# Three more q/k pairs by seven products, weights loaded by diagonals, head copies on ScalarE

## The chip, the cores and the metric

The kernel runs on one core of one Trainium2 chip. The metric is the device time of one execution in microseconds; lower is better. Three runs of the kernel before took 2038.73, 2040.16 and 2040.10 us, median 2040.1. One further execution was recorded by the hardware profiler.

Engines are called as in the profile: PE is TensorE's matrix multiplication and PEld its loading of the stationary operand, DVE is VectorE, ACT is ScalarE, POOL is GpSimd, SP is SyncE, which issues nearly all DMAs here.

## The reference

One layer of a hybrid block on x of 256 tokens by 4096 channels, everything in float32:

```
proj = rms_norm(x, norm_in_g) @ w_in                 # 4096 -> 14336
q, k, v, z_a, a_c, g_c, z_c = split(proj)            # each 2048 wide
y_a = rms_norm(chunked_attention(q, k, v, rel_table)) * silu(z_a)
u   = causal_depthwise_conv(a_c * sigmoid(g_c), w_dw) + b_dw      # 31 taps
y_c = rms_norm(silu(layer_norm(u)) @ w_pw + b_pw) * silu(z_c)
h   = x + concat(y_a, y_c) @ w_out                   # 4096 -> 4096
gate = sigmoid(rms_norm(h) @ w_ple_gate + b_ple_gate)  # 4096 -> 4096
out = rms_norm(h + gate * (p @ w_ple), final_g)
```

Attention has 16 heads of 128 channels; with 256 tokens every query's band of nine chunks of 64 reaches all earlier chunks. Almost all of the arithmetic is in the products with `w_in`, `w_out` and `w_ple_gate`.

## The kernel before

**Float32 by three products.** Each operand of a matmul is split into a high part, which the matmul's type holds exactly, and the rest. For weights `parts_of` (L198) does it: ACT copies the tile into `wh` (L203), DVE subtracts (L204) into `wl`. One product is then three matmuls: high by high, low by high, high by low. The stationary operand is a 128 x 128 block of the activations, the moving one 128 x 512 of the weights.

**Two columns at a time.** `mixed_product` (L326) computes, for both halves of the tokens (128 rows each) and for two weight columns of 512, the sum over 32 blocks of 128 channels, taken as 16 pairs. A list such as `early` (L319) gives the order of the pairs and says which are starred. A plain pair takes four products for each of its two blocks: 8 products, 24 matmuls. A starred pair is computed by a scheme of the Strassen and Winograd kind with seven products (P1 to P7), 21 matmuls. It takes sums of the weights, made on DVE for each pair (`ua`, L425 and L426; `ub`, L429 and L430) and split by `pair_parts` (L307) into `uh` and `ul`, and sums of the activations, made once and kept ("combined pairs", `xS` for x). Four helper sums P1, P5, P6, P7 stand in the temporary PSUM banks (`ps_tmp`, four in all) until the last starred pair of the product; `on_helpers` then adds them up on DVE and ACT (L466 to L470) and frees the banks. The other four sums are in `ps_acc`.

**Stages of the first half.** For g = 0 to 3: `glu_conv(g + 1)` (a and gate columns, then the convolution's taps as small DVE instructions put into a list `later`), `heads(g)` (q and k by one `mixed_product`, transposed by heads; v by `product`, L223; attention). `glu_conv(0)` goes ahead of all this and reads x. In the last group `layer_norm_swish` takes the place of the next `glu_conv`: it puts the layer norm over the convolution's output into `later`, with a mean (L742), a variance (L769) and a spread of the factor (L782) as small matmuls in temporary PSUM banks; the pointwise product then reads its result (`uS`, L798 and L799).

`fill` takes the given number of entries from `later` after each pair (`early_fills`, L322) or each two blocks of a `product` (`fills`). They are DVE's work between the weights' parts.

**Which pairs of x are combined.** Pairs 0, 2, 4 and 6 are combined early and kept in tiles of `upool`. In the last `glu_conv` two more, pairs 8 and 10, are made by `more_combinations` (L678) into tiles of the pool `act`; that product has the order `early_six` (L320). `act` has eight slots, which in the end hold four tiles of convolution output and four `y_a`. The q/k products of all four groups use `early`. With the end of the last group's q/k product the pools of the first half's sums are closed and the room goes to other tiles.

**Buffers.** Weight tiles `wt` have five slots, `wh` and `wl` three each, `uh` and `ul` two each. A load is issued by SP when the slot it takes has been read for the last time. For a starred pair the two loads are the two blocks, each with both columns (`two_columns`, L98): `w0` holds w00 and w01, `w1` holds w10 and w11. Outside the first half's glu and q/k products the two columns lie side by side in memory.

**Order.** Each engine runs its instructions in the order that a planner writes at compile time, by dependencies, program order and its own estimates of durations; where the program pins instructions they stay in program order. Nothing is reordered at run time, but for weight loads of PE.

**The q/k end of a group.** The four results of a q/k product are scaled on DVE (L491), transposed by heads on PE into temporary banks (`to_heads`, L822, L830) and copied out by DVE (L835) into `qT` and `kT`. The scores (L844, L845) read them after that, in the stream of the v product or behind it.

Of the kernel before, what the change touches and what calls it, by code (L numbers as in the profile page):

```python
# [16 lines left out]
P = 128  # L17
# [8 lines left out]
def hybrid_block(  # L26
# [71 lines left out]
    def two_columns(w, kb, col, apart):  # L98
# [4 lines left out]
            ap=[list(rows.ap[0]), [apart, 2], [1, NB]],  # L103
        )

    w_first = [wpool.tile([P, 2, NB], F32, tag="w", name="wt") for _ in range(2)]
    for j, col in enumerate((o_a, o_g)):
        nc.scalar.dma_start(w_first[0][:, j], w_in0[:P, col : col + NB])
# [86 lines left out]
    def part_tiles():  # L195
        return [wpool.tile([P, KC, NB], F32R, tag=tag, name=tag, bufs=3) for tag in ("wh", "wl")]

    def parts_of(wt, kc, tiles=None):  # L198
        if tiles is None:
            tiles = part_tiles()  # L200
        wh, wl = tiles
        made = (
            nc.scalar.copy(wh[:, :kc, :], wt[:, :kc, :]),  # L203
            nc.vector.tensor_tensor(  # L204
                wl[:, :kc, :], wt[:, :kc, :], wh[:, :kc, :].bitcast(F32), ALU.subtract
            ),
        )
        return (wh, wl), made
# [103 lines left out]
    def units(text):  # L312

        return [(int(u.rstrip("*")), u.endswith("*")) for u in text.split()]
# [3 lines left out]
    first = units("0 1 3 5 7 9 11 13 15 2* 8 4* 10 6* 12 14")  # L318
    early = units("1 3 5 7 0* 9 2* 11 4* 13 6* 15 8 10 12 14")  # L319
    early_six = units("1 3 5 7 0* 9 2* 11 4* 13 6* 15 8* 10* 12 14")  # L320

    early_fills = (4, 6, 7, 1, 5, 1, 5, 1, 5, 1, 2, 4, 6, 6, 6, 4)  # L322
    final = units("1 0* 3 2* 5 4* 6* 7 8* 9 10* 12* 11 13 14 15")
    late = units("1 3 5 7 9 11 13 15 0* 2 4* 6 8* 10* 12 14")

    def mixed_product(  # L326
# [67 lines left out]
        for n, (pair, seven) in enumerate(order):  # L394
            if n < done:
                continue
            if ahead:
                ahead(pair)
            wts = []
            for k in range(2):  # L400
                wt = wpool.tile([P, 2, NB], F32, tag="w", name="wt")
                nc.sync.dma_start(wt, two_columns(w, 2 * pair + k, col, apart))
                wts.append(wt)
            if n >= len(order) - n_left:
                for k in range(2):
                    tiles = left[2 * (n - len(order) + n_left) + k]
                    held.append((2 * pair + k, parts_of(wts[k], 2, tiles and tiles())[0]))
                fill(fills[n % len(fills)])
                continue
            if not seven:  # L410
                for k in range(2):
                    add_plain(n, k, *parts_of(wts[k], 2)[0])
                fill(fills[n % len(fills)])
                continue
            begins = not helper
            if begins:
                for name in ("P1", "P5", "P7", "P6"):
                    helper[name] = ps_tmp.tile([P, NB], F32, tag="tmp", name=f"acc_{name}")
                banks.update(helper)
            w0, w1 = wts  # L420
            ua = upool.tile([P, 2, NB], F32, tag="u", name="ua")
            ub = upool.tile([P, 2, NB], F32, tag="u", name="ub")
            plus = partial(nc.vector.tensor_tensor, op=ALU.add)
            w0h, w0l = parts_of(w0, 1)[0]
            plus(ua[:, 0], w0[:, 0], w0[:, 1])  # L425
            plus(ua[:, 1], w0[:, 1], w1[:, 1])  # L426
            uah, ual = pair_parts(ua)
            w1h, w1l = parts_of(w1, 2)[0]
            plus(ub[:, 0], ua[:, 0], w1[:, 1])  # L429
            plus(ub[:, 1], ub[:, 0], w1[:, 0])  # L430
            ubh, ubl = pair_parts(ub)
            first = len(made)

            def s_of(i):
                t, at = comb[pair] if isinstance(comb, dict) else (comb[pair // 4], pair % 4)
                return [t[:, at + i // 2, q, (i % 2) * P : (i % 2 + 1) * P] for q in range(2)]

            k0, k1 = 2 * pair, 2 * pair + 1
            add("P1", block(k0, 0), (w0h[:, 0], w0l[:, 0]), n, True)
            add("P5", s_of(1), (uah[:, 0], ual[:, 0]), n, True)  # L440
            add("P7", s_of(0), (uah[:, 1], ual[:, 1]), n, True)
            add("P2", block(k1, 0), (w1h[:, 0], w1l[:, 0]), n, True)
            add("P3", s_of(3), (w1h[:, 1], w1l[:, 1]), n, True)
            add("P6", s_of(2), (ubh[:, 0], ubl[:, 0]), n, True)
            add("P4", block(k1, 1), (ubh[:, 1], ubl[:, 1]), n, True)
            if begins and on_begin:
                on_begin()
            if begins:
                tc.add_manual_dep(
                    made[first].ins, last_transpose[0].ins.name,  # L450
                    mybir.DependencyInfo(mybir.DependencyClass.NoSync, mybir.DependencyReason.DATA),
                    reason="transposes before the helpers take their banks",
                )
            if n == last_seven:
                on_helpers(helper)
            fill(fills[n % len(fills)])
# [365 lines left out]
    def to_heads(st, name):  # L822

        t = spool.tile([P, GH, T], F32, tag="hd", name=name, bufs=5)
        for pair in range(GH // 2):
            pt = tmp_psum()
            for i in range(2):
                for h in range(NH):
                    b = 2 * pair + i
                    nc.tensor.transpose(  # L830
                        pt[:, i * T + h * P : i * T + (h + 1) * P],
                        st[:, h, b * P : (b + 1) * P],
                        ident,
                    )
            nc.vector.tensor_copy(  # L835
                t[:, 2 * pair : 2 * pair + 2, :], pt.rearrange("q (i t) -> q i t", t=T)
            )
        return t
# [40 lines left out]
    def heads(g):  # L879
        nonlocal more  # L880
        bias = spool.tile([P, GH, T], F32, tag="hd", name="bias", bufs=5)
        span = 2 * MAXR + 1
        nc.sync.dma_start(
            bias,
            bass.AP(
                tensor=rel_table.tensor,
                offset=rel_table.offset + g * GH * span + MAXR + P - (T - 1),
                ap=[[1, P], [span, GH], [1, T]],
            ),
        )  # L890
        nc.gpsimd.memset(bias[: P // 2, :, : P // 2], NEG)
        q, k = scaled_pair(w_in0, o_q + g * NB, o_k - o_q, early, r_x, (4,) if g == n_g - 1 else early_fills)
        qT, kT = to_heads(q, "qT"), to_heads(k, "kT")
        if g == n_g - 1:
            first_sums.close()
            more = pool("more", 4)
        accv = product(w_in0, o_v + g * NB, xT, KD)
        v = spool.tile([P, NH, NB], F32, tag="hd", name="v", bufs=5)
        for h in range(NH):
            nc.scalar.activation(v[:, h, :], accv[h], AF.Identity, scale=r_x[:, h : h + 1])  # L900
        attention(g, qT, kT, v, bias)
# [340 lines left out]
```

## Time and profile before

| | |
|---|---|
| median of three runs | 2040.1 us (2038.73 to 2040.16) |
| the profiled execution | 2040.09 us |
| its span, first to last instruction | 2038.1 us |
| mean granted clock of TensorE | 0.998 |
| ACT busy | 1180.8 us (58%) |
| HBM read | 406.39 MB |

The later stages by their start in the profiled execution: q/k of group 2 at 638 us, its v at 718, q/k of group 3 at 766, its v at 858, the pointwise product at 902, the gated products at 985, `w_out` at 1314, `w_ple_gate` at 1652.

In the profile's rows "out<-in" names the tile written and the tiles read; "x" and a number is a count; then come the busy time, the mean time of one in ns, the idle time of the engine ahead of them and what ended it. In a wait's row stand the waiting instruction, what ended the wait, the sum in us, how often, and the longest. In a timeline or a chain the first number is the start in us and the second the length in us; a row with "x3" joins three instructions. In a row of windows the columns are the stretch, its length, the busy time (and count) of PE, PEld, DVE, ACT and POOL, the granted clock, the DMA queues' mean share and GB/s. The chain follows the work that ended last.

### The profile page before, as it was taken

What the parts mean: (1) busy time and instruction counts of PE and PEld (TensorE: products, weight loads), DVE (VectorE), ACT (ScalarE), POOL (GpSimd) and SP (SyncE); (2) the same over time, 40 slices, a digit from 0 to 9 for tenths busy, and PEclk for the clock granted to TensorE, in tenths of its full rate; (3) what the DMA queues carried; (4) which work ended last, traced back from release to release, by engine and by line L of the source; (5) the groups of instructions that cost most, each with busy time, mean ns of one, the idle gap of its engine ahead of it and who ended that gap; (6) DMA issues with size and microseconds to landing.
All of it is one profiled execution on the core that took longest, in us unless ns stands there. A gap on an engine that the chain in (4) does not pass through costs nothing.

```text
span 2038.1 us, 26014 instructions
## 1 busy us (share of the span) xinstructions
PE 2020.2 (99%) x9112; PEld 1661.5 (82%) x9112; DVE 1892.9 (93%) x2700; ACT 1180.8 (58%) x1522; POOL 15.7 (1%) x19
## 2 busy tenths in 40 slices
PE   9999999999999999999999999999999999999997
PEld 7888888887888888888888887888888888888876
DVE  7999999899989998866999999999999999999998
ACT  7655535554555545565566566676565666655555
POOL 0000000000000000000100000000000000000000
PEclk9999999999999999999999999999999999999999
DMA  8666665666566665656666666676666656666765
GB/s 290 192 196 206 199 191 170 200 195 194 176 195 203 201 185 177 187 187 199 201 207 201 197 211 197 220 237 205 216 200 204 215 185 208 198 220 205 235 206 180
DMA packets 161852, 412.28 MB, mean 202 GB/s; under 512 B 12974, under 2 KB 16190, under 8 KB 161722
## 3 DMA queue, kind: packets, MB, share of 16 engines
q1 hardware_dynamic: 161072, 409.80, 63.6%
q8 instruction: 71, 1.16, 0.2%
q10 hardware_dynamic: 650, 0.84, 0.1%
q14 instruction: 59, 0.48, 0.1%
HBM read 406.39 MB, written 4.19 MB: 201 GB/s over the span
## 4 chain that ended last, share of the span: by engine, by line
PE 87%; DVE 9%; issue 2%; DMA 1%; ACT 1%; POOLq 0%; POOL 0%; ACTq 0%; DVEq 0%
PE acc L369 62%; PE acc_P L369 15%; PE acc L217 7%; DVE wl L204 3%; DVE cv L673 3%; PE tmp_ps L169 1%; DVE ul L204 1%; DMA wt<-in_w_in_dram 1%; PE tmp_ps L845 0%; PE tmp_ps L830 0%; PE tmp_ps L863 0%; DMA wt<-in_w_ple_dram 0%; PE tmp_ps L124 0%; PE tmp_ps L868 0%; DVE z L491 0%
## 5 line engine op out<-in xcount | busy, mean ns | idle before, releaser
L369 PE MATMUL acc<-wh,big_t 128*128 128x512 f32 x3846 | 1192.0, 392 | 1.5 <-DVE z L959 1.5
L203 ACT CAST wh<-wt 128x1024 fp32r<-128x1024 f32 (+1 forms) x737 | 715.7, 981 | 570.3 <-PE acc L369 348.9
L204 DVE TENSOR_TENSOR wl<-wt,wh 128x1024 fp32r<-128x1024 f32 (+1 forms) x737 | 824.7, 1130 | 61.1 <-ACT wh L203 57.2
L369 PEld LDWEIGHTS acc<-wh,big_t 128*128 128x128 f32 x3846 | 719.6, 188 | 150.2 <-ACT wh L203 1.9
L369 PE MATMUL acc<-wl,big_t 128*128 128x512 f32 x1923 | 741.9, 391 | 0.0
L369 PEld LDWEIGHTS acc<-wl,big_t 128*128 128x128 f32 x1923 | 360.6, 188 | 76.1 <-DVE wl L204 1.2
L673 DVE SCALAR_TENSOR_TENSOR cv<-uT,dw,cv 128x255 f32<-128x255 f32 (+20 forms) x480 | 204.6, 460 | 1.3
L203 ACT CAST uh<-ub 128x1024 fp32r<-128x1024 f32 x120 | 126.3, 1052 | 115.7 <-DVE ub L430 104.6
L369 PE MATMUL acc_P<-uh,big_t 128*128 128x512 f32 x594 | 182.2, 392 | 0.1
L217 PE MATMUL acc<-wh,big_t 128*128 128x512 f32 x560 | 173.1, 390 | 0.0
L203 ACT CAST uh<-ua 128x1024 fp32r<-128x1024 f32 x120 | 126.4, 1054 | 72.8 <-DVE ua L426 64.9
L204 DVE TENSOR_TENSOR ul<-ub,uh 128x1024 fp32r<-128x1024 f32 x120 | 146.3, 1219 | 7.0 <-ACT uh L203 5.7
L204 DVE TENSOR_TENSOR ul<-ua,uh 128x1024 fp32r<-128x1024 f32 x120 | 146.1, 1218 | 0.6 <-ACT uh L203 0.2
L369 PEld LDWEIGHTS acc_P<-uh,big_t 128*128 128x128 f32 x594 | 110.1, 188 | 26.2 <-ACT uh L203 4.1
L217 PEld LDWEIGHTS acc<-wh,big_t 128*128 128x128 f32 x560 | 104.8, 188 | 21.5
L369 PE MATMUL acc_P<-ul,big_t 128*128 128x512 f32 x297 | 114.5, 393 | 0.3 <-DVE ul L204 0.2
L217 PE MATMUL acc<-wl,big_t 128*128 128x512 f32 x280 | 109.2, 391 | 0.0
L425 DVE TENSOR_TENSOR ua<-wt 128x512 f32<-128x512 f32 x120 | 82.2, 685 | 22.1 <-DMA wt<-in_w_in_dram 17.3
L426 DVE TENSOR_TENSOR ua<-wt 128x512 f32<-128x512 f32 x120 | 82.0, 684 | 5.9 <-DMA wt<-in_w_in_dram 4.3
L430 DVE TENSOR_TENSOR ub<-ub,wt 128x512 f32<-128x512 f32 x120 | 82.2, 685 | 1.2
L429 DVE TENSOR_TENSOR ub<-ua,wt 128x512 f32<-128x512 f32 x120 | 82.0, 683 | 0.2
L369 PE MATMUL acc<-uh,big_t 128*128 128x512 f32 x240 | 74.4, 390 | 0.0
(223 smaller groups left out, 1423.0 us busy)
## 6 DMA issues: line engine op xcount, KB each, us to landing
wt<-in_w_in_dram SPq DMA_DIRECT2D x447, 512.0 KB, 4.1
wt<-in_w_out_dram SPq DMA_DIRECT2D x128, 512.0 KB, 4.3
wt<-in_w_ple_gate_dram SPq DMA_DIRECT2D x128, 512.0 KB, 4.2
wt<-in_w_pw_dram SPq DMA_DIRECT2D x32, 512.0 KB, 4.5
hc<-in_x_dram SPq DMA_DIRECT2D x8, 512.0 KB, 5.9
wt<-in_w_ple_dram SPq DMA_DIRECT2D x8, 512.0 KB, 4.7
xin<-in_x_dram SPq DMA_DIRECT2D x7, 512.0 KB, 8.2
out_dram<-hc SPq DMA_DIRECT2D x12, 256.0 KB, 2.5
```

What stands on the lines that cost most here:

```text
L169: nc.tensor.transpose(pt[:, i * T + h * P : i * T + (h + 1) * P], src[:, h, b * P : (b + 1) * P], ident,)
L203: nc.scalar.copy(wh[:, :kc, :], wt[:, :kc, :]),
L204: nc.vector.tensor_tensor(wl[:, :kc, :], wt[:, :kc, :], wh[:, :kc, :].bitcast(F32), ALU.subtract),
L217: nc.tensor.matmul(acc, a, b[:, k, :], start=kb == 0 and kind == 0, stop=kb == kblocks - 1 and kind == 2,)
L369: nc.tensor.matmul(banks[name], a, b, start=name not in begun, stop=final and ends[name] == n and kind == 2 and not (left and name in "P2 ...
L425: plus(ua[:, 0], w0[:, 0], w0[:, 1])
L426: plus(ua[:, 1], w0[:, 1], w1[:, 1])
L429: plus(ub[:, 0], ua[:, 0], w1[:, 1])
L430: plus(ub[:, 1], ub[:, 0], w1[:, 0])
L673: nc.vector.scalar_tensor_tensor(cv[:, i, PAD - k :], uT[:, i, : T + k - PAD], dw[:, b, k : k + 1], cv[:, i, PAD - k :], ALU.mult, ALU.add,)
```

## The change

1. The q/k product of group 2 takes the order `early_six` (six starred pairs in place of four), that of group 3 a new order `early_five` (five). They read the combined pairs 8 and 10 that the last `glu_conv` made; group 3 reads only pair 10, so that the tile of pair 8 becomes free for `y_a` of group 2.
2. Group 2's fills are 48 in the q/k product and 48 in the v product, in place of 64 and 32.
3. For starred pairs, in all products, the two loads are diagonals: `wd` holds w00 and w11, `wa` holds w01 and w10. `wd` is split whole (1024 columns), of `wa` only w10 (512). `ua` is made by one addition of 1024 columns, `wd` plus w01 repeated, in place of two of 512. The products come in the order P1, P3, P5, P7, P2, P6, P4 in place of P1, P5, P7, P2, P3, P6, P4. This part is computed with the same values as before.
4. The copies of `qT` and `kT` out of PSUM are made by ACT in place of DVE.

```diff
+    def diagonal(w, pair, col, apart, anti):
+
+        rows = w[2 * pair * P : (2 * pair + 1) * P, :]
+        n = rows.ap[0][0]
+        offset, step = (apart, P * n - apart) if anti else (0, P * n + apart)
+        return bass.AP(
+            tensor=rows.tensor, offset=rows.offset + col + offset,
+            ap=[list(rows.ap[0]), [step, 2], [1, NB]],
+        )
...
-    def parts_of(wt, kc, tiles=None):
+    def parts_of(wt, kc, tiles=None, k0=0):
...
+        ks = slice(k0, kc)
         made = (
-            nc.scalar.copy(wh[:, :kc, :], wt[:, :kc, :]),
+            nc.scalar.copy(wh[:, ks, :], wt[:, ks, :]),
             nc.vector.tensor_tensor(
-                wl[:, :kc, :], wt[:, :kc, :], wh[:, :kc, :].bitcast(F32), ALU.subtract
+                wl[:, ks, :], wt[:, ks, :], wh[:, ks, :].bitcast(F32), ALU.subtract
             ),
         )
...
+    early_five = units("1 3 5 7 0* 9 2* 11 4* 13 6* 15 10* 8 12 14")
...
+    third_fills = (4, 5, 6, 1, 4, 1, 4, 1, 4, 1, 2, 1, 1, 5, 4, 4)
...
-                nc.sync.dma_start(wt, two_columns(w, 2 * pair + k, col, apart))
+                nc.sync.dma_start(
+                    wt,
+                    diagonal(w, pair, col, apart, k) if seven
+                    else two_columns(w, 2 * pair + k, col, apart),
+                )
...
-            w0, w1 = wts
+            wd, wa = wts
...
-            w0h, w0l = parts_of(w0, 1)[0]
-            plus(ua[:, 0], w0[:, 0], w0[:, 1])
-            plus(ua[:, 1], w0[:, 1], w1[:, 1])
+            wdh, wdl = parts_of(wd, 2)[0]
+            plus(ua, wd, wa[:, :1].broadcast_to([P, 2, NB]))
             uah, ual = pair_parts(ua)
-            w1h, w1l = parts_of(w1, 2)[0]
-            plus(ub[:, 0], ua[:, 0], w1[:, 1])
-            plus(ub[:, 1], ub[:, 0], w1[:, 0])
+            wah, wal = parts_of(wa, 2, k0=1)[0]
+            plus(ub[:, 0], ua[:, 0], wd[:, 1])
+            plus(ub[:, 1], ub[:, 0], wa[:, 1])
             ubh, ubl = pair_parts(ub)
...
-            add("P1", block(k0, 0), (w0h[:, 0], w0l[:, 0]), n, True)
+            add("P1", block(k0, 0), (wdh[:, 0], wdl[:, 0]), n, True)
+            add("P3", s_of(3), (wdh[:, 1], wdl[:, 1]), n, True)
             add("P5", s_of(1), (uah[:, 0], ual[:, 0]), n, True)
             add("P7", s_of(0), (uah[:, 1], ual[:, 1]), n, True)
-            add("P2", block(k1, 0), (w1h[:, 0], w1l[:, 0]), n, True)
-            add("P3", s_of(3), (w1h[:, 1], w1l[:, 1]), n, True)
+            add("P2", block(k1, 0), (wah[:, 1], wal[:, 1]), n, True)
...
-            nc.vector.tensor_copy(
+            nc.scalar.copy(
                 t[:, 2 * pair : 2 * pair + 2, :], pt.rearrange("q (i t) -> q i t", t=T)
             )
...
-        q, k = scaled_pair(w_in0, o_q + g * NB, o_k - o_q, early, r_x, (4,) if g == n_g - 1 else early_fills)
+        order, fills = {
+            n_g - 2: (early_six, third_fills), n_g - 1: (early_five, (4,))
+        }.get(g, (early, early_fills))
+        q, k = scaled_pair(w_in0, o_q + g * NB, o_k - o_q, order, r_x, fills)
...
-        accv = product(w_in0, o_v + g * NB, xT, KD)
+        accv = product(w_in0, o_v + g * NB, xT, KD, fills=3 if g == n_g - 2 else 2)
```

## The prediction

> **What bounds the kernel now.** I read the page first, then the windows between start-up and tail, then TensorE's own waits, then the chain in order of time for one q/k group.
>
> ```profile
> span 2038.1 us, 26014 instructions
> ...
> PE 2020.2 (99%) x9112; PEld 1661.5 (82%) x9112; DVE 1892.9 (93%) x2700; ACT 1180.8 (58%) x1522; POOL 15.7 (1%) x19
> ```
>
> TensorE is busy 99%, VectorE 93%. Whether the first is a limit or a look is decided by the next two views: the sum of seven adjoining windows that cover 102 to 2000 us, and all that TensorE waited for in that stretch.
>
> ```profile
> sum 1898.00, PE 1893.91 PEld 1558.51 DVE 1780.33 ACT 1092.06 POOL 11.95; mean PE 270.56 PEld 222.64 DVE 254.33 ACT 156.01 POOL 1.71
> ...
> PE tmp_ps L830 <- DVE z L491: 1.6, 2, 1.3
> PE acc L369 <- DVE z L959: 1.5, 1, 1.5
> PE tmp_ps L868 <- DVE pT L865: 0.3, 1, 0.3
> PE acc_P L369 <- DVE ul L204: 0.2, 1, 0.2
> ```
>
> In 1898 us TensorE is without a matmul for 4.1 us, and waits explain 3.6 of them. So removing every stall is worth 4.1 us at most; the rest is the number of matmuls times their pace. The pace, from the last q/k group (start, length, count):
>
> ```profile
> 802.96 2.04 PE acc_P L369 x9
> 805.00 1.36 PE acc L369 x6
> 806.36 0.68 PE acc_P L369 x3
> 807.04 6.12 PE acc L369 x27
> ```
>
> One seven-product pair is 9 + 6 + 3 and the first 3 of the next row, 21 matmuls; a plain pair is 24. Each matmul takes 6.12/27 = 0.2267 us, the same in all four rows. That the others run ahead of TensorE is seen on ScalarE, which mostly waits for TensorE to give back a buffer:
>
> ```profile
> ACT wh L203 <- PE acc L369: 348.9, 263, 4.1
> ```
>
> **The matmuls (the main term).** `early` has four starred pairs, `early_six` six, `early_five` five. Group 2 gets two more, group 3 one: 3 pairs x 3 matmuls = 9 fewer, 9 x 0.2267 = **-2.04 us**. The kept pairs of x are the ones already made for the last glu group, so nothing is added to make them. The tiles they hold (pairs 8 and 10) are the slots that `y_a` of groups 2 and 3 take; those are written after each group's v product, when the last matmul on the kept tile is at least 44 us past (v takes 858 to 902 in the windows below). Cost nothing; without that distance it would be a wait in attention.
>
> **VectorE work.** Durations are in the groups by form; the interval from start to start in the timeline of VectorE matters more, since consecutive instructions overlap.
>
> ```profile
> L425 DVE TENSOR_TENSOR ua<-wt 128x512 f32<-128x512 f32 x120 | 82.2, 685 | 22.1 <-DMA wt<-in_w_in_dram 17.3 <-DMA wt<-in_w_out_dram 3.2 <-DMA wt<-in_w_ple_gate_dram 1.1
> ...
> L835 DVE COPY qT<-tmp_ps 128x512 f32<-128x512 f32 x8 | 5.1, 674 | 0.0
> ...
> L710 ACT COPY uT<-tmp_ps 128x512 f32<-128x512 f32 x8 | 4.3, 590 | 2.8 <-PE tmp_ps L705 2.8
> ...
> L750 DVE TENSOR_TENSOR lnsum<-lnsum,cv 128x1024 f32<-128x1024 f32 x2 | 2.4, 1216 | 0.0
> ...
> 722.65 3.48 DVE L204 TENSOR_TENSOR wl<-wt,wh 128x1024 fp32r<-128x1024 f32 x3
> ...
> 1773.48 0.68 DVE L426 TENSOR_TENSOR ua<-wt 128x512 f32<-128x512 f32 x1
> 1774.08 1.22 DVE L204 TENSOR_TENSOR wl<-wt,wh 128x1024 fp32r<-128x1024 f32 x1
> 1775.22 0.68 DVE L429 TENSOR_TENSOR ub<-ua,wt 128x512 f32<-128x512 f32 x1
> ```
>
> Three of 1024 take 3.48, so one occupies (3.48 - 1.21)/2 = 1.14 us; one of 512 occupies 0.60 (L426 to the next). The broadcast add (1024, one operand repeated) isn't in the trace; the nearest row, L750, is the same size and type, so 1.14, bounded by 1.20 (two of 512, no gain). A seven-product pair then goes from 3 x 1.14 + 5 x 0.60 = 6.42 to 4 x 1.14 + 3 x 0.60 = 6.36 us: -0.06 x 120 = -7 us over the kernel, between 0 and -18 (by whole durations, 0.685 + 0.684 - 1.216). The 16 head copies (0.674 each, 0.60 occupied) leave VectorE: -9.6. A plain pair is 2.28, so three pairs more by seven add 3 x (6.36 - 2.28) = +12.2. ScalarE: per pair the same one cast of 512 and three of 1024; 16 copies of 0.59 are added.
>
> None of this is on the path while VectorE stays ahead. The windows of groups 2 (q/k, v) and 3 (q/k, v):
>
> ```profile
> 638.00:718.00 80.00, 79.80 (x351) 65.32 (x351) 79.62 (x130) 40.52 (x44) 0.30 (x1) 1.00 0.67 206
> 718.00:766.00 48.00, 48.00 (x225) 39.70 (x223) 47.18 (x84) 21.27 (x24) 0.00 (x0) 1.00 0.61 180
> 766.00:854.00 88.00, 88.00 (x408) 72.44 (x407) 74.97 (x106) 51.29 (x74) 1.01 (x2) 1.00 0.61 191
> 858.00:902.00 44.00, 44.00 (x198) 36.50 (x197) 32.63 (x53) 29.68 (x49) 0.00 (x0) 1.00 0.61 190
> ```
>
> The fourth number is VectorE's busy time. Group 2 has 126.8 of 128; two more pairs are +8.2, its four copies -2.4, its merged adds -0.4: 5.4 us more than before in a stretch 1.36 us shorter. It fits only because the convolution taps can move on: they aren't needed before group 3's layer norm, and 766 to 854 has 13.0 us free. The new fills (48 + 48 for 64 + 32) move 16 taps from q/k to v. I take 0; if that cover is gone it is the last rival.
>
> **The order of products, waits on transfers.** P1, P3, P5, P7, P2, P6, P4: six matmuls (1.36 us) instead of three stand ahead of the first that needs `ua`'s parts. A `uh` buffer's release and its next use are five products apart before and after. 0, bounded by -0.2 (the row `acc_P <- ul`). The merged add waits for both transfers; `wd` is freed by L429's add instead of L426's:
>
> ```profile
> 1774.23 3.80 SPq L402 DMA_DIRECT2D wt<-in_w_ple_gate_dram  x2
> ```
>
> That load is issued right as L426's add ends; it would go out when L429's ends (1775.90), 1.7 us later. Behind it on SP's queue stands only the next load, which waits for L430's add in any case. Where transfers are late already (22.1 us ahead of L425 in the whole kernel) VectorE waits and TensorE doesn't, but for one wait of 1.5 us at L959. I take 0, between -0.5 and +1.6 (three borders inside the gated groups, each 1.14 - 0.60 later).
>
> The Trainium skill says in "DMA: Bandwidth & Descriptors", "Why small descriptors are slow (HBM only)", that each packet has a fixed overhead of some 3 cycles: by it, halves of rows cost a little more than whole rows. The trace's nearest rows are the two kinds of stage, q/k and glu (halves far apart) and w_out (halves side by side):
>
> ```profile
> 566.00:780.00 214.00, 213.80 (x971) 175.96 (x970) 197.75 (x304) 112.90 (x138) 0.61 (x2) 1.00 0.64 197
> ...
> 1314.00:1740.00 426.00, 426.00 (x1944) 353.26 (x1943) 406.86 (x560) 268.77 (x360) 0.69 (x1) 1.00 0.65 209
> ```
>
> 0.64 of the queues' time for 197 GB/s against 0.65 for 209: 4% more per byte, on a share of 0.65. No term.
>
> **The copies on ScalarE.** They wait for TensorE's transposes, and the next casts stand behind them. Three `wh` buffers hold 36 matmuls, 8.2 us, and ScalarE stands idle just there (group 2):
>
> ```profile
> 718.18 1.05 ACT L203 CAST wh<-wt 128x1024 fp32r<-128x1024 f32 x1 [1.66 <-PE acc L369]
> 722.81 1.05 ACT L203 CAST wh<-wt 128x1024 fp32r<-128x1024 f32 x1 [3.59 <-PE acc L217]
> ```
>
> Four copies of 0.59 need 2.4 of those 3.59 us. The scores that read them come after v in three groups and soon after the copies in one. I take +0.3, from 0 to +1.7 (one cast's wait ahead of a copy that TensorE's next scores need).
>
> **The wait at the head transposes.** In group 1 TensorE waits for the scaling, behind taps and L491 on VectorE:
>
> ```profile
> 493.00 1.59 DVE L673 SCALAR_TENSOR_TENSOR cv<-uT,dw,cv 128x228 f32<-128x228 f32 x4
> ...
> 494.51 2.71 DVE L491 SCALAR_TENSOR_TENSOR z<-acc,r_x,z 128x512 f32<-128x512 f32 x4
> 495.31 0.33 PE L830 MATMUL tmp_ps<-ident,z 128*128 128x128 f32 x1 [1.25 <-DVE z L491]
> ```
>
> That is 1.25 of the 1.6 us that TensorE waits at L830 in all; the other three groups have next to none. VectorE gets lighter there, but the order in which taps stand ahead of L491 is the planner's. From 0 to -1.6; I take half, -0.8.
>
> **Sum.** -2.04 - 0.8 + 0.3 + 0 = -2.5. The profiled execution took 2040.09 (span 2038.1 and 2.0 around it), the median of the three runs is 2040.1: **2037.5 us**, -0.13%. A measurement of this kernel can tell about 0.2% (4.1 us) from no change, so the likeliest verdict is "within".
>
> **Rivals.**
>
> A. **VectorE is the bound**, and TensorE's 99% are a look. Then the time follows VectorE's work: -7 - 9.6 + 12.2 = -4.4 by intervals, 2035.7; with the 2.04 of matmuls and 3.6 of waits gone together it is 2034.4. For it: 126.8 of 128 us busy in group 2. Against: the steady 0.2267, and that TensorE's idle time can't give more than 4.1. Its range is 2034.0 to 2036.0. The Trainium skill ("Perfetto Trace Analysis", "Identifying the Most-Contended Engine") holds that matmul busy time is no measure of TensorE's headroom and weight-load busy time is: by that, 82% would put VectorE's 93% first and speak for this rival; the trace's even matmul starts speak against it. 0.20.
>
> B. **The matmuls go, the time doesn't**: the 2.04 us come back as waits at group borders, as now at L959 (1.5) and L830 (1.6). 2040.1, within. For: VectorE is nearly full in group 2. Against: most borders have no wait. 0.12.
>
> C. **Slower: layer norm's reductions come late.** The helpers hold all four temporary banks until the last seven-product pair's sums are read; the mean's matmul (L742) follows at once:
>
> ```profile
> 823.36 2.04 PE acc_P L369 x9
> 825.39 0.64 PE tmp_ps L742 x2
> ...
> 850.53 0.34 PE tmp_ps L769 x4
> ...
> L799 DVE TENSOR_TENSOR big_t<-cv,big_t x16: 417/418/421, 877.0 to 885.6; 128x256 fp32r<-128x256 f32 x16
> ...
> 902.48 0.82 PE L369 MATMUL acc<-wh,big_t 128*128 128x512 f32 x2
> ```
>
> With `early_five` the last such pair is two places later (45 matmuls, 10.2 us). The splits that the pointwise product needs first start at 877.0, it starts at 902.5: 25 us to spare, so the delay alone costs nothing. But L742, L769 and L782 stand in TensorE's stream in order, and VectorE then has 5.4 (group 2's overflow) + 4.1 (one more pair) = 9.5 us more ahead of their inputs. If the planner places them without that lag, TensorE stands for it: 2040.1 - 2.0 + 9.5 = 2047.6. It beats the gain from a lag of 2.0 us, and shows as slower from 6.1. Against: 13.0 us free in 766 to 854 and 11.4 in 858 to 902. 0.12.
>
> **How the numbers follow.** Forecast 0.56 (own range 2035.5 to 2039.5, of which 0.08 below 2036.0), A 0.20, B 0.12, C 0.12. Faster by over 0.2%: 0.20 + 0.08 = 0.28. Slower: 0.12. Within: 0.60. The range goes from TensorE's floor, 2040.1 - 2.04 - 4.1 = 2034.0, to the forecast with none of the gains beside the matmuls and the upper bounds of transfers and copies, 2038.05 + 1.6 + 1.7 = 2041.4, and up to 2042.5 for part of C.
>
> **What would show it.** Right: 9103 matmuls instead of 9112, the pace still 0.2267; VectorE's busy time down by some 4 to 15 us with the span down by 2 to 3; one `ua` group of 1024 at about 1216 ns, x123; the rows for qT and kT on ACT at about 590 ns; waits of `acc_P` no longer than now. Wrong: TensorE idle over 4 us between 102 and 2000 us, waits of L742 or L769 for VectorE, longer waits of `ua` for transfers with TensorE waiting behind them, or a broadcast add far from 1216 ns.

## The result, and the profile after

The changed kernel takes **2057.32 us** (median of six runs, 2055.09 to 2061.72), the kernel before beside it 2039.63 (six runs, 2038.67 to 2041.17): ratio 1.009, 95% interval 1.0079 to 1.010. It is 17.7 us slower; forecast were 2.5 us less, and the range ended at 2042.5.

The profiled execution after has a span of 2058.1 us, 20.0 more than before. Its page begins so:

```profile
span 2058.1 us, 25938 instructions
...
PE 2029.7 (99%) x9103; PEld 1660.0 (81%) x9103; DVE 1889.1 (92%) x2579; ACT 1193.4 (58%) x1544; POOL 19.7 (1%) x19
```

The 9 matmuls are gone (9112 to 9103) and VectorE's work fell by 3.8 us. The time rose all the same, and TensorE still reads 99%. The windows of group 3 (q/k) and of `w_out`, and the sum of nine adjoining windows from 102 to 2018 us, show where it stands still:

```profile
774.00:868.00 94.00, 90.67 (x411) 73.59 (x410) 84.43 (x122) 53.62 (x78) 1.01 (x2) 0.98 0.58 179
...
1324.00:1670.00 346.00, 341.66 (x1524) 278.85 (x1523) 320.68 (x391) 207.07 (x264) 0.00 (x0) 1.00 0.65 207
...
sum 1916.00, PE 1901.37 PEld 1556.10 DVE 1774.98 ACT 1104.89 POOL 9.01; mean PE 211.26 PEld 172.90 DVE 197.22 ACT 122.77 POOL 1.00
```

TensorE is without a matmul for 14.6 us (4.1 before), 3.3 of it in group 3 and 4.3 in `w_out`, where it never stood still before. The busy time hides pauses of a few tenths between matmuls. Counted from start to start, all that lies beyond 0.2267 us adds up to 28.9 us before and 50.7 after over the whole kernel. These 21.8 us are nearly all of the 22.0 that have to be explained: the 20.0 by which the span grew, and the 2.04 saved. Waits of the same stretch:

```profile
DVE ua L442 <- DMA wt<-in_w_in_dram: 22.9, 22, 3.2
DVE ua L442 <- DMA wt<-in_w_out_dram: 12.9, 13, 2.2
PE acc L382 <- DVE wl L215: 7.2, 8, 2.8
PE acc L382 <- DVE hc L1060: 2.1, 1, 2.1
PE tmp_ps L846 <- DVE z L507: 1.9, 2, 1.5
```

The first two were 21.6 and 4.7 before (L425 and L426 together); with those for the gate product's loads all waits of `ua` for transfers went from 27.4 to 37.4. The new ones are TensorE's own, for `wl` (L215, the split) and for the sums at a border (L1060). And the merged add, in the groups by form, is what it was taken for:

```profile
L442 DVE TENSOR_TENSOR ua<-wt 128x1024 f32<-128x1024 f32 x123 | 150.0, 1220 | 37.8 <-DMA wt<-in_w_in_dram 22.9 <-DMA wt<-in_w_out_dram 12.9 <-DMA wt<-in_w_ple_gate_dram 1.6
```

How much later than before TensorE starts the first or last matmul into a helper bank (`acc_P`) of the same product, in us, in the changed kernel and in three of the experiments below (e2: diagonals alone; e4: all but the diagonals; e5: diagonals with one order set on VectorE):

| place | after | e2 | e4 | e5 |
|---|---|---|---|---|
| group 2, first of q/k | 5.1 | 3.7 | 0.2 | -1.4 |
| group 3, first of q/k | 6.9 | 5.2 | -0.8 | -1.2 |
| first of the gated products | 11.7 | 6.4 | 4.6 | -1.0 |
| last of the gated products | 10.8 | 6.7 | 3.1 | 1.3 |
| last of `w_out` | 18.3 | 13.9 | 3.0 | 4.7 |
| last of the gate product | 19.7 | 14.9 | 3.3 | 5.6 |

Two losses of different kind stand in it. One is spread over the stages before the gated products and over `w_out`, 7.2 us in `w_out` alone and next to none in the gated products (e2). The other is inside group 3 (e4).

### The profile page after: what moved, and what is told of

Read it like the earlier page. It is cut to its first block, busy times and chain, and to the rows that moved or that the text cites. A ratio compares the mean times of both kernels' runs of the same rounds, so it can differ in the third digit from the quotient of the medians.

```text
span 2058.1 us, 25938 instructions
## 1 busy us (share of the span) xinstructions
PE 2029.7 (99%) x9103; PEld 1660.0 (81%) x9103; DVE 1889.1 (92%) x2579; ACT 1193.4 (58%) x1544; POOL 19.7 (1%) x19
## 4 chain that ended last, share of the span: by engine, by line
PE 84%; DVE 9%; issue 3%; DMA 2%; ACT 1%; POOLq 0%; POOL 0%; ACTq 0%; DVEq 0%
PE acc L382 59%; PE acc_P L382 14%; PE acc L228 8%; DVE wl L215 3%; DVE cv L689 2%; DVE ul L215 1%; PE tmp_ps L179 1%; DMA wt<-in_w_in_dram 1%; DMA wt<-in_w_out_dram 1%; DVE ua L442 1%; PE tmp_ps L846 0%; DVE ub L445 0%; ACT uh L214 0%; PE tmp_ps L861 0%; DMA wt<-in_w_ple_gate_dram 0%
## 5 line engine op out<-in xcount | busy, mean ns | idle before, releaser
L214 ACT CAST wh<-wt 128x1024 fp32r<-128x1024 f32 x737 | 717.7, 979 | 528.3 <-PE acc L382 359.3
L215 DVE TENSOR_TENSOR wl<-wt,wh 128x1024 fp32r<-128x1024 f32 x737 | 823.8, 1129 | 69.2 <-ACT wh L214 65.9
L689 DVE SCALAR_TENSOR_TENSOR cv<-uT,dw,cv 128x255 f32<-128x255 f32 (+24 forms) x480 | 203.1, 462 | 1.2
L442 DVE TENSOR_TENSOR ua<-wt 128x1024 f32<-128x1024 f32 x123 | 150.0, 1220 | 37.8 <-DMA wt<-in_w_in_dram 22.9
L215 DVE TENSOR_TENSOR ul<-ub,uh 128x1024 fp32r<-128x1024 f32 x123 | 149.9, 1219 | 15.7 <-ACT uh L214 15.1
L215 DVE TENSOR_TENSOR ul<-ua,uh 128x1024 fp32r<-128x1024 f32 x123 | 149.8, 1218 | 0.8 <-ACT uh L214 0.3
L228 PEld LDWEIGHTS acc<-wh,big_t 128*128 128x128 f32 x560 | 105.5, 189 | 21.6
L445 DVE TENSOR_TENSOR ub<-ua,wt 128x512 f32<-128x512 f32 x123 | 84.3, 685 | 1.1
L382 PE MATMUL acc_P<-wh,big_t 128*128 128x512 f32 x246 | 75.7, 389 | 0.0
```

The costliest lines, as they stand in the source:

```text
L214: nc.scalar.copy(wh[:, ks, :], wt[:, ks, :]),
L215: nc.vector.tensor_tensor(wl[:, ks, :], wt[:, ks, :], wh[:, ks, :].bitcast(F32), ALU.subtract),
L228: nc.tensor.matmul(acc, a, b[:, k, :], start=kb == 0 and kind == 0, stop=kb == kblocks - 1 and kind == 2,)
L382: nc.tensor.matmul(banks[name], a, b, start=name not in begun, stop=final and ends[name] == n and kind == 2 and not (left and name in "P2 ...
L442: plus(ua, wd, wa[:, :1].broadcast_to([P, 2, NB]))
L445: plus(ub[:, 0], ua[:, 0], wd[:, 1])
```

## The experiments

Each was timed in alternation with the kernel before, which had medians of 2039.94 (e1 to e4), 2039.54 (e5 to e8), 2040.10 (e9 to e12) and 2039.68 us (e13 to e15).

### The parts alone: e1 to e4

The edits are the parts of the diff shown above: e1 is the kernel before with parts 1 and 2 (orders and fills), e2 with part 3 (the diagonals), e3 with part 4 (`nc.scalar.copy` for the head copies); e4 is e1 and e3 together.

> Parts 1 and 2 alone (two more starred pairs in group 2, one more in group 3, the new fills); loads, product order and head copies as before. Theory T (the diagonals lose the most): 9 matmuls fewer, -2.0 us, and some +4 to +6 of late weight parts in groups 2 and 3, so +2 to +4 us, 2042 to 2044. Rival O (the extra pairs by seven overload VectorE): +12 to +18, 2052 to 2058. Rival S (nothing alone, only the three together): -2 to +1, 2037.5 to 2040.5.

> Part 3 alone (diagonal loads, one merged add, the new order of the seven products); orders, fills and head copies as before. Theory T: the 0.6 us up to group 2, some of what group 3 lost, and all of what w_out and the gate product lost (7.6 and 0.9 us): +11 to +16, 2050 to 2056, with the waits of ua for w_out's loads near 13 us as in the changed kernel (before: 3.2). Rival O: +1 to +4. Rival S: -1 to +2.

> Part 4 alone (the 16 head copies on ScalarE). Theory T: within 1 us of before (2038.5 to 2040.5), the wait at the head transposes of group 1 no longer than before. Rival A (the copies stand ahead of casts that TensorE needs): +3 to +8, with waits of TensorE on uh or wh in groups 0 to 3.

> Parts 1, 2 and 4, without part 3: the changed kernel with loads by blocks, two adds of 512 and the old order of the seven products. Theory T: +1 to +5, 2041 to 2045, with the waits of ua for transfers as before (22 us in all). Rival O: +12 to +18. Rival A: 4 us or more above e1.

| | us | against before | 95% interval of the ratio |
|---|---|---|---|
| e1 | 2042.56 | +2.6 | 1.0005 to 1.0022 |
| e2 | 2055.10 | +15.2 | 1.0063 to 1.0090 |
| e3 | 2038.71 | -1.2 | 0.9984 to 1.0002 |
| e4 | 2041.41 | +1.5 | 1.0000 to 1.0017 |

The parts add: 2.6 + 15.2 - 1.2 = 16.6 of the 17.7. The diagonals are the loss; the extra pairs cost a little where they should save 2; for the copies no cost is seen.

### The loop through a weight slot

The timeline of VectorE in `w_out` of the changed kernel, one plain and one seven-product pair, with the one issue of a load on SP's queue (the row SPq) that fills the next `wa`:

```profile
1470.41 1.22 DVE L442 TENSOR_TENSOR ua<-wt 128x1024 f32<-128x1024 f32 x1 [0.60 <-DMA wt<-in_w_out_dram]
1471.55 2.35 DVE L215 TENSOR_TENSOR wl<-wt,wh 128x1024 fp32r<-128x1024 f32 x2
1473.82 0.69 DVE L445 TENSOR_TENSOR ub<-ua,wt 128x512 f32<-128x512 f32 x1
1474.42 1.22 DVE L215 TENSOR_TENSOR ul<-ua,uh 128x1024 fp32r<-128x1024 f32 x1
1475.56 1.22 DVE L215 TENSOR_TENSOR wl<-wt,wh 128x1024 fp32r<-128x1024 f32 x1
...
1481.59 1.23 DVE L442 TENSOR_TENSOR ua<-wt 128x1024 f32<-128x1024 f32 x1 [1.19 <-DMA wt<-in_w_out_dram]
...
1476.80 0.38 SPq L415 DMA_DIRECT2D wt<-in_w_out_dram  x1
```

There are five slots, and four loads to a plain and a seven-product pair: so the second load of the *next* seven-product pair takes the slot of the *first* load of this one, `wd`. Its last reader is the split at 1475.56, behind two splits of the plain pair. The load goes out as it ends, at 1476.80, 6.39 us after `ua` began, and the next `ua` starts when it has landed, 4.79 us later. The loop is 11.18 us; TensorE eats the two pairs, 45 matmuls, in 10.20. What VectorE loses at each turn it takes from its lead, until `wl` or a border's sums come late. In e2, which has the diagonals alone, the handing on is seen (VectorE, then TensorE):

```profile
1478.32 1.22 DVE L442 TENSOR_TENSOR ua<-wt 128x1024 f32<-128x1024 f32 x1 [1.19 <-DMA wt<-in_w_out_dram]
...
1480.19 2.35 DVE L215 TENSOR_TENSOR wl<-wt,wh 128x1024 fp32r<-128x1024 f32 x2
...
1481.46 0.50 PE L382 MATMUL acc<-wl,big_t 128*128 128x512 f32 x1 [1.03 <-DVE wl L215]
```

`ua` waits for its transfer, the plain pair's splits stand behind it, and TensorE, which has started the plain pair, waits for the first of them. All seven pauses of TensorE above 0.4 us for `wl` in e2 between 102 and 2018 us have this form, 7.3 us together.

The same place before (`w0` is the first load, and `ua` is made by two adds, of which L426 needs both):

```profile
1459.19 0.68 DVE L426 TENSOR_TENSOR ua<-wt 128x512 f32<-128x512 f32 x1
...
1463.81 0.68 DVE L204 TENSOR_TENSOR wl<-wt,wh 128x512 fp32r<-128x512 f32 x1
...
1469.31 0.68 DVE L426 TENSOR_TENSOR ua<-wt 128x512 f32<-128x512 f32 x1
...
1464.52 0.33 SPq L402 DMA_DIRECT2D wt<-in_w_out_dram  x1
```

The same loop, from the add that needs both transfers (1459.19) to the load that takes `w0`'s slot: 5.33 us. The transfer lands 4.30 us later, and the next such add does not wait for it. Even with the 4.79 of the changed kernel the loop is 10.1, just inside 10.20. The change made the part up to the load 1.06 longer: the add is 1.22 instead of 0.68 and the first load's split 1.22 instead of 0.69. The loop was followed in `w_out` alone; in the gated products the waits of `ua` for transfers went down, from 9.6 to 6.6 us in e2.

e5 takes the loop apart without touching a load or a buffer:

```diff
-            wdh, wdl = parts_of(wd, 2)[0]
-            plus(ua, wd, wa[:, :1].broadcast_to([P, 2, NB]))
+            (wdh, wdl), split = parts_of(wd, 2)
+            tc.add_manual_dep(
+                plus(ua, wd, wa[:, :1].broadcast_to([P, 2, NB])).ins, split[1].ins.name,
+                mybir.DependencyInfo(mybir.DependencyClass.NoSync, mybir.DependencyReason.DATA),
...
+            )
```

> Part 3 alone as in e2, but with one order set on VectorE: wd's split stands ahead of ua's add, where the planner of e2 mostly put it four to six instructions behind it. No instruction, load or buffer is added. Theory L (a loop through a weight slot: ua needs both transfers, the second takes the slot that wd leaves 5.2 us later, and the transfer takes 4.1 to 5.1 us, together about the 10.2 us that TensorE needs for a plain and a seven-product pair): wd's slot is free 1.8 us after ua begins, so the waits of ua for transfers fall from 37 us to under 10 and the time from 2055 to 2038 to 2042. Rival P (the 2 KB packets, or the transfers, are slower by themselves): the waits and the time stay, 2052 to 2057. Rival M (the products' new order or the merged add): 2050 to 2056.

Measured 2045.72 us, +6.2 (1.0019 to 1.0041): 9.0 of e2's 15.2 are back, and the time is above the 2038 to 2042 expected. Its VectorE in `w_out`, and the load:

```profile
1463.20 1.22 DVE L215 TENSOR_TENSOR wl<-wt,wh 128x1024 fp32r<-128x1024 f32 x1 [0.77 <-ACT wh L214]
1464.35 1.22 DVE L443 TENSOR_TENSOR ua<-wt 128x1024 f32<-128x1024 f32 x1
1465.60 0.69 DVE L449 TENSOR_TENSOR ub<-ua,wt 128x512 f32<-128x512 f32 x1
...
1474.55 1.22 DVE L443 TENSOR_TENSOR ua<-wt 128x1024 f32<-128x1024 f32 x1
...
1466.35 0.38 SPq L415 DMA_DIRECT2D wt<-in_w_out_dram  x1
```

The load goes out 2.00 us after `ua` begins, `ua` follows `ua` by TensorE's own 10.20, and no wait of `ua` for a transfer is left between 102 and 2018 us (e2: 38.0 us). So the waits came from that loop, and of TensorE's own waits for `wl`, 6.1 us in e2, 0.4 are left. The other 6 us of the loss did not come from it; see e13.

e6 and e7 tried two rivals: the merged add (e2 with two adds of 512, `w00 + w01` and `w11 + w01`), and the diagonals' packets of 2 KB (before, with each seven-product pair's columns stored in swapped order, so that no two packets join; the splits and adds take the other half).

The edit of e6, against e2:

```diff
-            plus(ua, wd, wa[:, :1].broadcast_to([P, 2, NB]))
+            plus(ua[:, 0], wd[:, 0], wa[:, 0])
+            plus(ua[:, 1], wd[:, 1], wa[:, 0])
```

The load of e7, against before:

```diff
-                nc.sync.dma_start(wt, two_columns(w, 2 * pair + k, col, apart))
+                nc.sync.dma_start(
+                    wt, two_columns(w, 2 * pair + k, *((col + apart, -apart) if seven else (col, apart)))
+                )
```

> Part 3 alone as in e2, but ua by two adds of 512 (w00 + w01, w11 + w01) in place of the merged one. Theory L: both still need both transfers, so as e2 within 3 us, 2051 to 2058. Rival M (the merged add with a repeated operand costs it): 2038 to 2043. The adds alone make it 0.06 x 120 = 7 us more of VectorE's work.

> The kernel before with the two columns of each seven-product pair's blocks stored in swapped order, so that every row of a load goes in two packets of 2 KB in w_out, the gate product and the gated ones, as with the diagonals; nothing else. Theory L: 2039 to 2042, no new waits above 5 us. Rival P: 2047 or more, with most of the loss in w_out (7.2 us in e2).

e6: 2054.22, +14.7 (1.0059 to 1.0084). e7: 2040.17, +0.6 (0.9993 to 1.0011). The page of e7 has 184124 packets, as that of e2, against 161852 before. Neither the add's form nor the packets are the cause. The Trainium skill ("DMA: Bandwidth & Descriptors", "Why small descriptors are slow (HBM only)") gives each packet a fixed overhead of some 3 cycles; e7 shows that here it doesn't reach the time.

### Two that went another way: e9 and e10

e9 is the kernel before with one order set, the add that needs both transfers ahead of the one that needs only the first:

```diff
-            plus(ua[:, 0], w0[:, 0], w0[:, 1])
-            plus(ua[:, 1], w0[:, 1], w1[:, 1])
+            second = plus(ua[:, 1], w0[:, 1], w1[:, 1])
+            tc.add_manual_dep(
+                plus(ua[:, 0], w0[:, 0], w0[:, 1]).ins, second.ins.name,
+                mybir.DependencyInfo(mybir.DependencyClass.NoSync, mybir.DependencyReason.DATA),
...
+            )
```

> The kernel before with block loads and the old products; only the two adds of ua change places on VectorE, so that the first one (now w01 + w11) needs both transfers, as the merged add of the diagonals does. Theory L (the loop closes because the first add needs both transfers): ua waits for transfers 30 us or more (before: 22), TensorE's waits grow, 2043 to 2052. Rival D (what hurts is the diagonals' late release of wd, not that both transfers are needed): 2038.5 to 2041.

The time is in the range of L, 2048.88, +8.8 (1.0031 to 1.0056), but not for L's reason: `ua` waits 14.0 us for transfers, less than before. Needing both transfers at once does not close the loop by itself. What grew most in the list of waits is TensorE's waiting for the splits of the sums (`ul`): its weight loads (PEld) stand 10.4 us for them in e9, 4.4 before:

```profile
PEld acc_P L369 <- DVE ul L204: 10.4, 25, 1.8
```

One order set on VectorE costs 8.8 us, with the same instructions and loads.

e10 is e2 with both reads of `wd` (its split and the add into `ub`) ordered ahead of `ua`'s split:

```diff
+            for ins in (split[1], added):
+                tc.add_manual_dep(
+                    parts[1].ins, ins.ins.name,
+                    mybir.DependencyInfo(mybir.DependencyClass.NoSync, mybir.DependencyReason.DATA),
...
+                )
```

> Part 3 alone, as e2, with another order on VectorE than e5's: wd's split and its add into ub stand ahead of ua's split (ul), so wd's slot is free some 2.3 to 4.5 us after ua begins (e5: 1.8, e2: 5.2), and ua itself does not wait for the cast of wd. Theory L: little waiting of ua for transfers (under 15 us; e2 has 37). If the 6 us that e5 still loses come from uh and ul, made just in time because ua stands behind wd's split, these go: 2038 to 2043. Rival (they come from the new products' order): 2044 to 2048.

2056.26, +16.2 (1.0066 to 1.0094), and 48.0 us of waits of `ua`. The expectation was wrong about the planner: it kept the order asked for, but put the plain pair's splits between `ua` and those reads (VectorE's timeline of e10 in `w_out`, and the load):

```profile
1472.07 1.23 DVE L442 TENSOR_TENSOR ua<-wt 128x1024 f32<-128x1024 f32 x1 [0.33 <-DMA wt<-in_w_out_dram]
1473.22 2.36 DVE L215 TENSOR_TENSOR wl<-wt,wh 128x1024 fp32r<-128x1024 f32 x2
1475.49 0.68 DVE L443 TENSOR_TENSOR ub<-ua,wt 128x512 f32<-128x512 f32 x1
...
1476.82 1.22 DVE L215 TENSOR_TENSOR wl<-wt,wh 128x1024 fp32r<-128x1024 f32 x1
...
1482.95 1.22 DVE L442 TENSOR_TENSOR ua<-wt 128x1024 f32<-128x1024 f32 x1 [2.05 <-DMA wt<-in_w_out_dram]
...
1478.06 0.38 SPq L415 DMA_DIRECT2D wt<-in_w_out_dram  x1
```

The load goes out as `wd`'s split (1476.82) ends, 5.99 us after `ua`, not 2.3 to 4.5, the loop is 10.88 us, and the waits are there. That is what the loop gives for such a release, though not the test that was meant.

### The products' order: e13 and e14

P3 back in its old place behind P2, with e5's order on VectorE (e13) and without it (e14):

```diff
-            add("P3", s_of(3), (wdh[:, 1], wdl[:, 1]), n, True)
             add("P5", s_of(1), (uah[:, 0], ual[:, 0]), n, True)
...
             add("P2", block(k1, 0), (wah[:, 1], wal[:, 1]), n, True)
+            add("P3", s_of(3), (wdh[:, 1], wdl[:, 1]), n, True)
```

> e5 (part 3 alone, wd split ahead of ua) with the product P3 back in its old place, behind P2. Theory C (the 6 us that e5 still loses come from the chain of wd's cast, wd's split, ua, uh, ul, all one behind the other, so that P5 and P7 find uh and ul just ready): P5 now stands 3 matmuls, 0.68 us, earlier, so as e5 or worse, 2045 to 2052. Rival Q (the new order of the products costs it): 2038 to 2043.

> e2 (part 3 alone, VectorE's order left to the planner) with P3 back in its old place. Theory L (the loop through wd's slot): the loss stays, 2050 to 2060, with more than 25 us of ua waiting for transfers. Rival Q (the new order of the products costs it): 2045 or less.

e13: 2045.59, +5.9 (1.0018 to 1.0040), as e5. e14: 2057.15, +17.5 (1.0073 to 1.0100). The products' order is not the cause of either loss. What is left of e5 is told by its list of waits. First the two rows of e2:

```profile
DVE wl L215 <- ACT wh L214: 50.9, 60, 1.5
PEld acc_P L382 <- DVE ul L215: 5.7, 17, 0.9
```

The same two of e5:

```profile
DVE wl L215 <- ACT wh L214: 78.1, 114, 2.9
PEld acc_P L382 <- DVE ul L215: 11.1, 32, 0.5
```

VectorE now waits for ScalarE's cast of `wd` before it may make `ua`, and TensorE gets `uh` and `ul` just in time: of its pauses between 1010 and 2000 us, counted from start to start (15.9, before 9.0), 9.9 stand at matmuls on `uh` and `ul` (before 3.2). That is a reading of the trace; no run took this chain away alone.

### Group 3: e8 and e11

The timelines of VectorE and TensorE in group 3 of the changed kernel (L770 centers the convolution's output, L778 squares it, L483 to L486 add up the helpers):

```profile
845.22 3.10 DVE L770 TENSOR_TENSOR cv<-cv,mu 128x256 f32<-128x256 f32 x9
848.24 0.68 DVE L483 TENSOR_TENSOR z<-acc_P,z 128x512 f32<-128x512 f32 x1
...
853.96 1.22 DVE L778 TENSOR_TENSOR sq<-sq 128x1024 f32<-128x1024 f32 x1
...
855.43 2.35 DVE L215 TENSOR_TENSOR wl<-wt,wh 128x1024 fp32r<-128x1024 f32 x2
...
851.89 1.98 PE L382 MATMUL acc<-wh,big_t 128*128 128x512 f32 x8
856.71 1.76 PE L382 MATMUL acc<-wl,big_t 128*128 128x512 f32 x4 [2.84 <-DVE wl L215]
```

For 10.2 us VectorE does nothing but centers, squares and the helpers' sums; the next pair's `wl` stands behind them, and TensorE waits 2.84. e4 has the same wait, and its windows show that more follows:

```profile
845.00:850.00 5.00, 2.16 (x6) 1.47 (x5) 4.91 (x7) 3.78 (x5) 0.00 (x0) 0.76 0.10 11
850.00:855.00 5.00, 5.00 (x14) 3.85 (x14) 3.67 (x5) 0.12 (x1) 0.00 (x0) 0.56 0.90 306
```

The granted clock is 0.56: 14 matmuls stand in 5 us where 22 go at 0.2267, so some 1.8 us are lost in that window beside the wait. e1, with the same orders, has the same wait of 2.84 us and no such dip (its windows stand at the end); there TensorE loses 2.6 us between the first of group 3's q/k and the first of the gated products, in e4 5.4. e8 leaves group 3 as it was before (e4 with `early` there); e11 only moves its fifth pair one place forward, so that the helpers are free 5.4 us earlier:

The edit of e8, against e4:

```diff
-    early_five = units("1 3 5 7 0* 9 2* 11 4* 13 6* 15 10* 8 12 14")
...
-        order, fills = {
-            n_g - 2: (early_six, third_fills), n_g - 1: (early_five, (4,))
-        }.get(g, (early, early_fills))
+        order, fills = {n_g - 2: (early_six, third_fills), n_g - 1: (early, (4,))}.get(g, (early, early_fills))
```

That of e11, against e4:

```diff
-    early_five = units("1 3 5 7 0* 9 2* 11 4* 13 6* 15 10* 8 12 14")
+    early_five = units("1 3 5 7 0* 9 2* 11 4* 13 6* 10* 15 8 12 14")
```

> The kernel before with early_six and the new fills in group 2 and the copies on ScalarE, but group 3 with its four starred pairs as before. Theory N (what the extra pairs lose, they lose in group 3: with the helpers' sums two places later the layer norm's centers and squares stand ahead of the weights' last parts, 3.0 us of TensorE and a dip of the clock after it): 6 matmuls fewer, -1.4, and e3's -1.2: 2037 to 2039, with no wait of TensorE over 1 us and no dip of the clock in group 3. Rival (the loss is VectorE's overload from group 2): 2041 or more.

> As e4 (parts 1, 2 and 4), but group 3's fifth starred pair stands ahead of pair 15: the helpers are free one place (24 matmuls, 5.4 us) earlier. Theory N (late helpers put the layer norm's centers and squares ahead of the weights' parts): the 3.0 us of TensorE at 845 us and the clock's dip shrink or go, 2037 to 2040. Rival (more work by VectorE in group 3 by itself): as e4, 2041 to 2042.

e8: 2037.83, -1.7 (0.9982 to 0.9999). e11: 2037.16, -2.9 (0.9977 to 0.9995), 4.4 better than e4 relative to before. Here are the same two windows of e11:

```profile
845.00:850.00 5.00, 5.00 (x24) 4.08 (x23) 5.00 (x5) 3.07 (x3) 0.00 (x0) 1.00 0.81 237
850.00:855.00 5.00, 5.00 (x25) 4.09 (x24) 3.68 (x8) 2.11 (x2) 0.70 (x1) 1.00 0.78 261
```

The longest wait for `wl` in group 3 is 0.4 us and the clock stays whole. VectorE has the same work in both; the place of one pair decides.

### Diagonals in the first half alone: e12 and e15

e12 is e8 with the diagonals and e5's order, but only where the two columns lie apart (glu and q/k, `if apart != NB`); the second half loads by blocks. e15 adds e11's fifth pair.

```diff
-                    diagonal(w, pair, col, apart, k) if seven
+                    diagonal(w, pair, col, apart, k) if seven and apart != NB
...
+            if apart != NB:
+                (wdh, wdl), split = parts_of(wd, 2)
...
+            else:
+                w0h, w0l = parts_of(wd, 1)[0]
...
```

> e8 (early_six in group 2 alone, copies on ScalarE) with the diagonals and e5's order in the products whose two columns lie apart (glu and q/k) alone; gated, w_out and gate products by blocks as before. In e5 the first half ended 1.1 us ahead of before, the second lost 6: so e8's 2037.8 less 1 to 2, 2035.5 to 2037.5, if the two gains add; 2037.5 to 2039 if the same waits are removed twice.

> e12 with group 3's fifth starred pair added in e11's place (ahead of pair 15): 3 matmuls fewer, -0.7 us against e12's 2036.0, so 2035.3 (2034.5 to 2036.5), if the layer norm still finds its bank in time; 2038 or more if the helpers are late again.

e12: **2035.97**, -4.1 (0.9972 to 0.9990). e15: 2037.04, -2.6 (0.9978 to 0.9996). Both are faster than the kernel before; among e8, e11, e12 and e15 the intervals overlap. e15 came out above the 2034.5 to 2036.5 expected: its trace has a wait of 1.2 us for `wl` in group 3, where e12 has none, more than the 0.68 that three matmuls save. That this wait is the reason is not shown.

## Why the prediction was wrong

**The step that failed** is "The order of products, waits on transfers": 0, between -0.5 and +1.6. Alone it measures +15.2 (e2). Three things in it were wrong.
- The release of `wd` was priced once, from one pair of the gate product: 1.7 us later, "Behind it on SP's queue stands only the next load". The gate product lost only 1.3 us (from the last of `w_out` to its own last in the table). The release was never followed round: slot, load, transfer, `ua`, and back to the slot. Followed round in `w_out` it is 5.33 us plus a transfer of 4.30 before, in a turn of 10.20, and 11.18 with the change.
- The last reader of `wd` was taken to be the add L445. In `w_out` it is the split of all 1024 columns, which the planner put behind two others.
- "VectorE waits and TensorE doesn't" was true of the 22.1 us before (27.4 with those of L426): TensorE's own waits were 3.6 us. It was no bound on longer ones: with 37.4 us of waits TensorE's pauses grew by 21.8.

Of the 15.2 us, the loop has 9.0 (e5). For the other 6 there is the reading of e5's waits and no run.

A reading at the start failed too: "removing every stall is worth 4.1 us at most" is taken from busy time. From start to start the pauses before were 28.9 us over the kernel, start-up included. And it says nothing of how far they can grow: one order set on VectorE (e9) cost 8.8 us.

**VectorE's work** came as worked out where it was a duration: the add 1.220 (expected 1.216), 123 of them, busy time -3.8 us, just short of the 4 to 15 named. "None of this is on the path while VectorE stays ahead" failed in group 3.

**The matmuls**: 9103, at 0.2267, as forecast. e8 (six fewer, -1.7 us) and e11 (nine fewer, -2.9), which also have the copies on ScalarE, are in line with it.

**The copies on ScalarE**: +0.3 (0 to 1.7) was forecast; e3 measures -1.2 (0.9984 to 1.0002), near enough to nothing. **The wait at the head transposes**, -0.8 forecast, stayed (1.9 after 1.6). **The halves of rows**: no term, and e7 gives none.

**The rivals.** A, VectorE as the bound by its sum, falls: its work fell by 3.8 us and the time rose by 17.7. B had the matmuls given back as waits at borders. TensorE's waits for `z` and `hc` there went only from 3.1 to 4.3 us; what grew is inside the products, the waits for `wl` above all (7.2, before none). C had the place and the cause of the smaller loss, the helpers' late sums in group 3, at a chance of 0.12, but not its form: L758 (L742 before), the mean's matmul, has no wait in the list but 0.4 us of its weight load. What waited was the next `wl`, because the centers and squares came to stand ahead of it, and the clock's dip, where it came, was not in the price. In time (+1.5 for e4) C's place is real and its 7.5 too much.

Of the signs named as "wrong", two came: TensorE idle for more than 4 us, and longer waits of `ua` for transfers with TensorE waiting behind them.

## What to carry to other kernels

A buffer that is loaded again is a loop: from the first instruction that needs the transfer, through the last reader of the slot that the *next* such transfer takes, through the issue and the transfer, and back. Add it up in us and hold it against the consumer's own period, also where an edit only changes which instruction reads last; a share of busy time and a list of harmless waits say nothing about it. And on VectorE, busy 92 to 93% here, the place of a few instructions in its order was worth 4 to 9 us (e5, e9, e11), while the 3.8 us of work that the change took off it brought nothing.

## What the runs showed of the hardware

A short stall of TensorE can cost more than itself. In e4, behind the wait for `wl` in group 3 (2.84 us), TensorE's timeline has matmuls 0.43 us apart, twice the usual 0.2267 (two start between 850.12 and 850.97):

```profile
848.24 2.08 PE L371 MATMUL acc<-wl,big_t 128*128 128x512 f32 x4 [2.84 <-DVE wl L204]
850.12 1.05 PE L371 MATMUL acc<-wh,big_t 128*128 128x512 f32 x2
850.97 0.63 PE L371 MATMUL acc<-wl,big_t 128*128 128x512 f32 x1
```

The changed kernel shows it also at the head transposes of group 1, where TensorE was busy 1.13 of 3 us; the granted clock of the next 4 us is 0.59:

```profile
495.00:498.00 3.00, 1.13 (x6) 0.52 (x5) 3.00 (x7) 1.04 (x1) 0.00 (x0) 1.00 0.65 208
498.00:502.00 4.00, 4.00 (x20) 3.58 (x20) 4.00 (x6) 2.25 (x4) 0.00 (x0) 0.59 0.21 38
```

The Trainium skill ("TensorE: Matmul & The Clock Gate", "Part 1: The HAM clock gate") has the clock halved after an idle window of about 3.4 us. The halving is seen here; the idle time ahead of it is shorter than that in both places (2.84 us, and 1.54 and 0.33), and the measurement decides.

The stall need not bring the dip. e1 has the same wait of 2.84 us, up to 848.86, and its clock stays whole:

```profile
843.00:848.00 5.00, 3.03 (x14) 2.18 (x12) 4.91 (x11) 4.19 (x6) 0.00 (x0) 1.00 0.00 0
848.00:853.00 5.00, 4.14 (x18) 3.41 (x19) 5.00 (x6) 2.19 (x3) 0.00 (x0) 1.00 0.55 170
```

What decides it no run here shows. The dips lasted 3.4 us twice in the changed kernel (498.7 to 502.1 and 857.1 to 860.5 us, granted clock 0.50), and 6.8 us once in e4 (847.6 to 854.4). At half the pace that is an estimated 1.7 us lost in each of the first two, 3.4 of the 20.0 by which that execution's span grew. e2 has no dip between 102 and 2018 us, so they are not what the diagonals cost.
